# Two joint weight units per feed-forward block: weight loads chained in their written order, and the third weight sum made by VectorE instead of by DMAs

## The chip, the cores and the metric

The kernel runs on one core of a Trainium2 chip. The metric is the device time of one execution in microseconds (us). The program is recorded once, and a scheduler then decides in which order each engine's instructions stand; each engine and each DMA queue works through its own list strictly in that order.

## The reference, cut to what matters

A decoder trunk of four layers on 256 tokens with 1024 channels. Each layer has a feed-forward block (SwiGLU), a token mixer, and a second feed-forward block, so eight feed-forward blocks in all, and these hold most of the weights:

```python
def swiglu(x, wg, wu, wd):
    return (jax.nn.silu(x @ wg) * (x @ wu)) @ wd
...
    for i in range(DEPTH):
        h = rms_norm(x, ffn_norm[i, 0])
        x = x + 0.5 * swiglu(h, ffn_w_gate[i, 0], ffn_w_up[i, 0], ffn_w_down[i, 0])
        ...
        h = rms_norm(x, ffn_norm[i, 1])
        x = x + 0.5 * swiglu(h, ffn_w_gate[i, 1], ffn_w_up[i, 1], ffn_w_down[i, 1])
```

All of it is fp32, with `D_FF` 2816.

## The kernel before, in words

The 256 tokens are two tiles of 128 (t = 0, 1). Weights stream from HBM once. A unit `g` is 512 columns of gate and up weights, and it arrives as two loads of 1 MB (`raw<-gu`); a unit `d` is 512 rows of the down matrix, also two loads of 1 MB (`raw<-dn`). All loads of this kind go through SyncE's DMA queue into three buffers of 1 MB (tag `raw`, `bufs=3`), so a load waits until the last reader of the buffer that it takes over is done, and every later entry of that queue waits behind it.

Each weight is used as two numbers: ScalarE writes the rounded upper part (`hi`), VectorE the rest (`lo` = raw minus hi). That is a split, done in quarters of 128 x 1024, into nine buffers of either kind (`HALVES = 9`); `split_some` hands out the quarters, one or two per tick of the program, and a quarter waits until TensorE has read what its buffers held. Every product is three matmuls (lines 292 to 294, in joint units 474 to 476): hi times upper activations, hi times lower, lo times upper.

The order of units in a block is `FFN_ORDER`: g0 to g3, d0, g4, g5, d1, g6, g7, d2, g8, g9, d3, g10, d5, d4. The pairs (g4, g5) and (g8, g9) are **joint units** (`JOINT = (4, 8,)`): the four weight blocks b11, b21, b12, b22 and both token tiles are multiplied in seven products of half size instead of eight (a Strassen scheme), for which sums of weight blocks are needed:

- t1 = b12 + b11. SyncE loads b12 in two halves (`start`), then GpSimd starts two more DMAs that add b11 to it in flight (`add`, with `accum_op`).
- t2 = t1 + b22, by VectorE in place (line 233).
- t3 = b12 + b22, made like t1 by DMAs: SyncE loads b12 a second time, GpSimd's DMAs add b22.
- t4 = t2 + b21, by VectorE in place over t2.

The sums lie in buffers of tag `a4` (`bufs=9`, half a megabyte each, shared with other tiles). `split_joint` queues the quarters in the order b11, t1, t2, t3, b21, t4, b22; b11, b22 and b21 each hold one of the three `raw` buffers until their last reader is done. `joint` then multiplies: b11, t2, t1, t3, b21, t4, b22.

Behind each joint unit comes a `d` unit, d1 or d3. Its two loads, here called **dn1 and dn2**, take the buffers that b11 and b21 leave. In the scheduled program TensorE multiplies part of that unit for tile 0 (`acc`, lines 292 to 294) after the fifth product and before t4 and b22. The block's values `th` (line 1248 on ScalarE, 1249 on VectorE) and `h` (line 1254) are turned on TensorE (line 1262).

Of the kernel before, what the change touches and what calls it, by code (L numbers as in the profile page):

```python
# [80 lines left out]
class Net:  # L81
    def __init__(self, ctx, tc, a, layers):
        self.tc, self.nc, self.a = tc, tc.nc, a
        self.layers = layers

        def pool(name, **k):
            return ctx.enter_context(tc.tile_pool(name=name, bufs=1, **k))

        self.cp, self.wp, self.ap, self.sp = pool("const"), pool("weights"), pool("act"), pool("small")
        self.ps = pool("psum", space=PSUM)  # L90
        self.units, self.raw, self.parts = [], {}, {}
        self.n_fetch = self.n_split = 0
        self.seq, self.due, self.queue, self.memkv = [], [], [[], []], {}
        self.ticks = 0
        self.jobs, self.open = [], []
        self.extra = []
        self.st, self.splits = [{}, {}], []
        self.plan()
# [30 lines left out]
    def plan(self):  # L129
# [21 lines left out]
        def both(n):  # L151
            self.seq += [(n, 3)] if self.units[n][0] == "j" else [(n, 0), (n, 1)]

        for j, i in enumerate(self.layers):
# [23 lines left out]
            for u in range(n, len(self.units)):  # L178
                both(u)

    def fetch(self):
        u = self.n_fetch
        if u >= len(self.units):
            return
        self.n_fetch += 1
        if self.units[u][0] == "j":
            self.fetch_joint(u)
            return
        self.raw[u] = []
        for ap in self.units[u][1]:  # L190
            n = ap.shape[1]
            r = self.wp.tile([128, n], F32, name="raw", tag="raw", bufs=3)
            self.nc.sync.dma_start(r, ap)
            self.raw[u].append(r)

    def fetch_joint(self, u):

        nc = self.nc
        b11, b21, b12, b22 = self.units[u][1]
        half = lambda ap, q: ap[:, 1024 * q:1024 * q + 1024]  # L200
        raw = self.raw[u] = {}

        def plain(name, ap):
            raw[name] = self.wp.tile([128, 2048], F32, name="raw", tag="raw", bufs=3)
            nc.sync.dma_start(raw[name], ap)

        def start(name):
            raw[name] = [self.t4([128, 1024], "sum") for _ in range(2)]
            for q in range(2):
                nc.sync.dma_start(raw[name][q], half(b12, q))  # L210

        def add(name, ap):
            for q in range(2):
                nc.gpsimd.dma_start(raw[name][q], half(ap, q), accum_op=OP.add)

        plain("b11", b11)
        start("t1")
        add("t1", b11)
        plain("b22", b22)
        start("t3")  # L220
        add("t3", b22)
        plain("b21", b21)

    def split_joint(self, u):
        nc = self.nc
        raw, parts = self.raw.pop(u), self.parts[u]
        parts.update({n: [] for n in ("b11", "t1", "t2", "t3", "b21", "t4", "b22")})
        half = lambda n, q: raw[n][:, 1024 * q:1024 * q + 1024] if n[0] == "b" else raw[n][q]

        def quarter(name, src, q, plus):  # L230
            x = half(src, q)
            if plus:
                nc.vector.tensor_add(x, x, half(plus, q))
            hi = self.wp.tile([128, 1024], F32R, name="hi", tag="hi", bufs=HALVES)
            lo = self.wp.tile([128, 1024], F32R, name="lo", tag="lo", bufs=HALVES)
            nc.scalar.activation(hi, x, AF.Copy)  # L236
            nc.vector.tensor_sub(lo, x, hi.bitcast(F32))  # L237
            parts[name].append((hi, lo))

        for name, src, plus in (("b11", "b11", None), ("t1", "t1", None), ("t2", "t1", "b22"), ("t3", "t3", None),  # L240
                                ("b21", "b21", None), ("t4", "t1", "b21"), ("b22", "b22", None)):
            for q in range(2):
                self.splits.append((u, lambda name=name, src=src, q=q, plus=plus: quarter(name, src, q, plus)))
# [1350 lines left out]
```

## Time and profile before

| | |
|---|---|
| Time, median of 3 runs | 2109.27 us (2106.8 to 2116.53) |
| The profiled execution, own time | 2109.68 us |
| Its span, first to last instruction | 2107.9 us |
| TensorE busy | 2028.5 us (96%) |
| VectorE busy | 1520.9 us (72%) |
| ScalarE busy | 1114.2 us (53%) |
| Moved by DMA | 402.11 MB, mean 191 GB/s |
| TensorE's mean granted clock | 0.985 |

The time of the profiled execution is its span and 1.8 us around it. Matmuls overlap in the pipeline, so a busy TensorE can still be slowed; the number of matmuls in a stretch and the distance from one start to the next tell more than its busy time.

### The profile page before, as it was taken

The page shows a single profiled execution, that of the slowest core. Times are in us where ns is not written, and L with a number is a line of the kernel's source. Part 1 is how long each engine was busy: PE and PEld are TensorE (multiplying, and loading weights), DVE is VectorE, ACT ScalarE, POOL GpSimd, SP SyncE. Part 2 cuts the span into 40 slices and gives each one's busy share as a digit, 9 for nine tenths or more (in the row PEclk, how much of TensorE's full clock was granted, in tenths as well). Part 3 has the DMA queues.
Part 4 walks back from the last instruction along what each step waited for, and adds up shares of the span by engine and source line. Part 5 has one row for each costly group of instructions (what it writes and reads, how often), then busy time and mean ns, then how long its engine had stood idle before and what let it go on. Part 6 is the DMA issues. An engine that isn't in the chain of part 4 may idle for free.

```text
span 2107.9 us, 25369 instructions
## 1 busy us (share of the span) xinstructions
PE 2028.5 (96%) x9486; PEld 1628.5 (77%) x9486; DVE 1520.9 (72%) x2209; ACT 1114.2 (53%) x1562; POOL 227.7 (11%) x349
## 2 busy tenths in 40 slices
PE   8899999899989999989998999999899989999899
PEld 6677777778867887868777788877788778778687
DVE  7677757778767787867777876667786868658675
ACT  6455655446545555545545554544555545545453
POOL 0100411100100022100000112210000100301000
PEclk9999999999999999999999999999999999999999
DMA  7855535865683533684577443137744774436843
GB/s 260 261 189 220 180 120 200 241 218 200 213 245 143 205 110 120 234 246 145 218 235 242 182 173 130 64 121 235 241 179 180 231 248 181 159 120 215 249 149 126
DMA packets 66988, 402.11 MB, mean 191 GB/s; under 512 B 7600, under 2 KB 8016, under 8 KB 28080
## 3 DMA queue, kind: packets, MB, share of 16 engines
q1 hardware_dynamic: 56304, 364.54, 47.2%
q0 software_dynamic: 9408, 33.97, 8.3%
q10 hardware_dynamic: 1152, 1.97, 0.3%
q8 instruction: 75, 1.23, 0.2%
q14 instruction: 49, 0.40, 0.1%
HBM read 399.40 MB, written 1.05 MB: 190 GB/s over the span
## 4 chain that ended last, share of the span: by engine, by line
PE 74%; DMA 12%; DVE 8%; ACT 3%; issue 2%; POOL 1%; SPq 0%; ACTq 0%; DVEq 0%; POOLq 0%
PE pg L292 8%; PE pg L294 8%; PE pg L293 8%; PE acc L293 7%; PE acc L294 6%; PE acc L292 6%; DMA sum<-gu 5%; DVE lo L237 4%; DMA raw<-gu 3%; PE p L292 3%; DMA raw<-dn 3%; PE p L293 3%; PE p L294 3%; DVE lo L265 2%; PE pT L1262 2%
## 5 line engine op out<-in xcount | busy, mean ns | idle before, releaser
L265 DVE TENSOR_TENSOR lo<-raw,hi 128x1024 fp32r<-128x1024 f32 (+3 forms) x516 | 615.6, 1217 | 175.1 <-ACT hi L264 168.5
L264 ACT ACTIVATE hi<-raw 128x1024 fp32r<-128x1024 f32 (+3 forms) x516 | 527.1, 1046 | 273.0 <-DMA raw<-gu 79.0
L292 PE MATMUL pg<-hi,sh 128*128 128x512 f32 x896 | 354.8, 396 | 4.4 <-ACT hi L1347 3.4
L293 PE MATMUL pg<-lo,sh 128*128 128x512 f32 x896 | 350.7, 391 | 0.7 <-DVE lo L1348 0.7
L294 PE MATMUL pg<-hi,sl 128*128 128x512 f32 x896 | 349.8, 390 | 0.0
L292 PE MATMUL acc<-hi,hTh 128*128 128x512 f32 x704 | 286.0, 410 | 34.9 <-ACT hi L264 34.9
L293 PE MATMUL acc<-lo,hTh 128*128 128x512 f32 x704 | 288.0, 413 | 4.6 <-DVE lo L265 4.4
L294 PE MATMUL acc<-hi,hTl 128*128 128x512 f32 x704 | 282.4, 405 | 0.0
L236 ACT ACTIVATE hi<-sum 128x1024 fp32r<-128x1024 f32 x128 | 132.3, 1057 | 165.4 <-PE acc L294 88.9
L237 DVE TENSOR_TENSOR lo<-sum,hi 128x1024 fp32r<-128x1024 f32 x128 | 154.2, 1226 | 77.6 <-ACT hi L236 75.9
L292 PEld LDWEIGHTS pg<-hi,sh 128*128 128x128 f32 x896 | 168.3, 188 | 39.2 <-ACT hi L1347 4.3
L293 PEld LDWEIGHTS pg<-lo,sh 128*128 128x128 f32 x896 | 168.5, 188 | 35.4 <-DVE lo L1348 2.5
L294 PEld LDWEIGHTS pg<-hi,sl 128*128 128x128 f32 x896 | 168.2, 188 | 35.6 <-DVE sl L1370 0.4
L292 PEld LDWEIGHTS acc<-hi,hTh 128*128 128x128 f32 x704 | 135.8, 193 | 68.6 <-ACT hi L264 38.4
L293 PEld LDWEIGHTS acc<-lo,hTh 128*128 128x128 f32 x704 | 136.0, 193 | 42.0 <-DVE lo L265 14.2
L294 PEld LDWEIGHTS acc<-hi,hTl 128*128 128x128 f32 x704 | 136.4, 194 | 27.9 <-DVE hTl L1264 0.2
L1248 ACT ACTIVATE th<-pg,rh 128x256 f32<-128x256 f32 x128 | 60.3, 471 | 179.4 <-PE pg L294 174.0
L1249 DVE SCALAR_TENSOR_TENSOR th<-th,pg 128x256 f32<-128x256 f32 x128 | 53.5, 418 | 107.6 <-ACT th L1248 107.1
L237 DVE TENSOR_TENSOR lo<-raw,hi 128x1024 fp32r<-128x1024 f32 x96 | 114.9, 1226 | 18.9 <-ACT hi L236 18.9
L292 PE MATMUL p<-hi,sh 128*128 128x512 f32 (+4 forms) x320 | 125.2, 391 | 0.3 <-DVE dq_b L529 0.3
L294 PE MATMUL p<-hi,sl 128*128 128x512 f32 (+4 forms) x320 | 121.2, 379 | 0.0
L293 PE MATMUL p<-lo,sh 128*128 128x512 f32 (+4 forms) x320 | 120.9, 378 | 0.0
(344 smaller groups left out, 3185.0 us busy)
## 6 DMA issues: line engine op xcount, KB each, us to landing
raw<-gu SPq DMA_DIRECT2D x158, 1024.0 KB, 5.0
raw<-dn SPq DMA_DIRECT2D x88, 1024.0 KB, 4.9
sum<-gu SPq DMA_DIRECT2D x64, 512.0 KB, 7.6
sum<-gu POOLq DMA_DIRECT2D x64, 512.0 KB, 11.5
raw<-ret SPq DMA_DIRECT2D x20, 1024.0 KB, 4.8
raw<-wout SPq DMA_DIRECT2D x16, 1024.0 KB, 4.8
raw<-mkv SPq DMA_DIRECT2D x8, 1024.0 KB, 4.8
raw<-nsa SPq DMA_DIRECT2D x6, 1024.0 KB, 4.9
```

Of the source, the lines that this page charges most:

```text
L236: nc.scalar.activation(hi, x, AF.Copy)
L237: nc.vector.tensor_sub(lo, x, hi.bitcast(F32))
L264: nc.scalar.activation(hi, src, AF.Copy)
L265: nc.vector.tensor_sub(lo, src, hi.bitcast(F32))
L292: mm(out, ah, bh, start=start, stop=False)
L293: mm(out, ah, bl, start=False, stop=False)
L294: mm(out, al, bh, start=False, stop=stop)
L1248: nc.scalar.activation(th, p[:, :256], AF.Tanh, scale=rh_)
L1249: nc.vector.scalar_tensor_tensor(th, th, 1.0, p[:, :256], op0=OP.add, op1=OP.mult)
L1262: nc.tensor.transpose(c[:, k], h[:, k * 128:k * 128 + 128], self.ident)
```

## The change

Three things are changed. Loads of weights by SyncE go through a helper, `load`, that ties each of them behind the one before, with a dependency that orders the scheduler and makes no semaphore wait. In a joint unit the loads are written in another order (t1's halves first, then b11, b22, b21). And t3 is no longer made by DMAs: VectorE makes it as t2 minus b11, in two instructions of 128 x 1024, into buffers that are allocated when the quarter is split. The order of matmuls is not fixed by anything (the helper `behind` serves loads alone, and `self.last` is not used).

```diff
+        self.last = self.loaded = None
...
+    def load(self, dst, src):
+
+        self.nc.sync.dma_start(dst, src)
+        i = self.nc.cur_bb.bb.instructions[-1]
+        if self.loaded is not None:
+            self.behind(i, self.loaded)
+        self.loaded = i
+
+    def behind(self, i, j):
+
+        self.tc.add_manual_dep(
+            i, j.name, mybir.DependencyInfo(mybir.DependencyClass.NoSync, mybir.DependencyReason.DATA),
+            reason="in order")
...
-            self.nc.sync.dma_start(r, ap)
+            self.load(r, ap)
...
-        plain("b11", b11)
         start("t1")
         add("t1", b11)
+        plain("b11", b11)
         plain("b22", b22)
-        start("t3")
-        add("t3", b22)
         plain("b21", b21)
...
             x = half(src, q)
-            if plus:
+            if name == "t3":
+                raw.setdefault("t3", []).append(self.t4([128, 1024], "sum"))
+                nc.vector.tensor_sub(raw["t3"][q], x, half("b11", q))
+                x = raw["t3"][q]
+            elif plus:
                 nc.vector.tensor_add(x, x, half(plus, q))
...
-        for name, src, plus in (("b11", "b11", None), ("t1", "t1", None), ("t2", "t1", "b22"), ("t3", "t3", None),
+        for name, src, plus in (("b11", "b11", None), ("t1", "t1", None), ("t2", "t1", "b22"), ("t3", "t1", None),
```

**SyncE's queue around the first joint unit of the third feed-forward block (layer 1).** Before (`raw_4701` is b11, `sum_4703` and `sum_4704` t1, `sum_4711` and `sum_4712` t3, `raw_4709` b22, `raw_4717` b21; `raw_4800` and `raw_4802` are dn1 and dn2, and the four `sum_52..` between and behind these are t1 and t3 of the second joint unit):

```order
L205 DMA raw_4701<-gu 128x2048
L210 DMA sum_4703<-gu 128x1024
L210 DMA sum_4704<-gu 128x1024
L210 DMA sum_4711<-gu 128x1024
L210 DMA sum_4712<-gu 128x1024
L205 DMA raw_4709<-gu 128x2048
L205 DMA raw_4717<-gu 128x2048
L193 DMA raw_4800<-dn 128x2048
L210 DMA sum_5225<-gu 128x1024
L210 DMA sum_5226<-gu 128x1024
L210 DMA sum_5233<-gu 128x1024
L193 DMA raw_4802<-dn 128x2048
```

The same place with the change (all of these loads are now recorded at line 184; `sum_4693` and `sum_4694` are t1, `raw_4699`, `raw_4701` and `raw_4703` are b11, b22 and b21, `raw_4786` and `raw_4788` dn1 and dn2, and the last five are the units g6 and g7 and the first load of d2):

```order
L184 DMA sum_4693<-gu 128x1024
L184 DMA sum_4694<-gu 128x1024
L184 DMA raw_4699<-gu 128x2048
L184 DMA raw_4701<-gu 128x2048
L184 DMA raw_4703<-gu 128x2048
L184 DMA raw_4786<-dn 128x2048
L184 DMA raw_4788<-dn 128x2048
L184 DMA raw_4893<-gu 128x2048
L184 DMA raw_4895<-gu 128x2048
L184 DMA raw_5096<-gu 128x2048
L184 DMA raw_5098<-gu 128x2048
L184 DMA raw_5139<-dn 128x2048
```

The four loads for the second joint unit have left their places around dn2. Two of them are gone, and the other two stand behind both loads of d2, directly ahead of the second unit's b11:

```order
L184 DMA raw_5141<-dn 128x2048
L184 DMA sum_5213<-gu 128x1024
L184 DMA sum_5214<-gu 128x1024
L184 DMA raw_5219<-gu 128x2048
L184 DMA raw_5221<-gu 128x2048
```

(`raw_5141` is the second load of d2, `sum_5213` and `sum_5214` are t1 of the second joint unit, the two behind them its b11 and b22; GpSimd's queue has two additions per joint unit, and had four.)

**VectorE at the same joint unit.** Before (L233 adds b22 or b21 to t1, L237 writes a lower part, `hTl` belongs to the block's activations):

```order
L237 TENSOR_TENSOR lo_4881<-sum_4703,hi_4880 128x1024
L233 TENSOR_TENSOR sum_4704<-sum_4704,raw_4709 128x1024
L1264 TENSOR_TENSOR hTl_4849<-pT_4872,hTh_4848 128x512
L233 TENSOR_TENSOR sum_4703<-sum_4703,raw_4717 128x1024
L237 TENSOR_TENSOR lo_4886<-sum_4704,hi_4885 128x1024
L237 TENSOR_TENSOR lo_4902<-sum_4711,hi_4901 128x1024
L237 TENSOR_TENSOR lo_4924<-sum_4712,hi_4923 128x1024
```

With the change (lines 250 and 254 are 233 and 237 of before, 1281 is 1264; line 247 is the subtraction):

```order
L254 TENSOR_TENSOR lo_4867<-sum_4693,hi_4866 128x1024
L250 TENSOR_TENSOR sum_4694<-sum_4694,raw_4701 128x1024
L1281 TENSOR_TENSOR hTl_4835<-pT_4858,hTh_4834 128x512
L247 TENSOR_TENSOR sum_4887<-sum_4693,raw_4699 128x1024
L247 TENSOR_TENSOR sum_4911<-sum_4694,raw_4699 128x1024
L250 TENSOR_TENSOR sum_4693<-sum_4693,raw_4703 128x1024
L254 TENSOR_TENSOR lo_4872<-sum_4694,hi_4871 128x1024
```

Both subtractions stand ahead of the first addition of b21, and everything behind them keeps its order. They are the last readers of b11's buffer, which dn1 takes over. TensorE's list keeps its order but for some exchanges among `acc` matmuls and transposes behind a joint unit.

## Rows read from the trace of the kernel before

**Rows 1.** The page: the length of the profiled execution, and its first part, the busy time of each engine with its share of the span and its number of instructions.

```profile
span 2107.9 us, 25369 instructions
...
PE 2028.5 (96%) x9486; PEld 1628.5 (77%) x9486; DVE 1520.9 (72%) x2209; ACT 1114.2 (53%) x1562; POOL 227.7 (11%) x349
```

**Rows 2.** The waits of TensorE over the whole span. Columns: engine, what it was to write and the line, the engine and line that it waited for, then the total in us, how often, and the longest one in us.

```profile
PE acc L292 <- ACT hi L264: 34.9, 8, 5.7
PE pT L1262 <- DVE h L1254: 20.7, 15, 5.1
PE acc L293 <- DVE lo L265: 4.4, 12, 0.5
```

**Rows 3.** The timeline of TensorE at the first joint unit of the third feed-forward block (layer 1). Columns: start in us, duration in us, engine, line, operation, output and inputs, count; in brackets the idle time just before and what ended it.

```profile
589.02 0.44 PE L1262 MATMUL pT<-ident,h 128*128 128x128 f32 x2 [2.00 <-DVE h L1254]
...
612.31 0.40 PE L294 MATMUL acc<-hi,hTl 128*128 128x512 f32 x1
618.19 0.80 PE L292 MATMUL acc<-hi,hTh 128*128 128x512 f32 x1 [5.48 <-ACT hi L264]
619.45 0.80 PE L293 MATMUL acc<-lo,hTh 128*128 128x512 f32 x1 [0.47 <-DVE lo L265]
...
623.03 0.42 PE L474 MATMUL pg<-hi,op 128*128 128x512 f32 x1
```

**Rows 4.** The same joint unit in stretches of 10 us. Columns: stretch, its length, then for each engine the busy time with the number of instructions, then the granted TensorE clock, the share of the DMA engines and GB/s.

```profile
600.00:610.00 10.00, 10.00 (x45) 8.23 (x44) 9.39 (x10) 6.84 (x8) 1.73 (x2) 1.00 0.82 206
610.00:620.00 10.00, 4.06 (x14) 2.67 (x13) 3.54 (x4) 2.37 (x3) 0.86 (x1) 0.81 1.04 315
620.00:630.00 10.00, 10.00 (x38) 8.00 (x37) 7.87 (x13) 5.05 (x6) 0.86 (x1) 0.85 1.03 352
```

**Rows 5.** The span of the core and its mean granted TensorE clock over the whole execution (1 is the upper of its two levels).

```profile
core 0: 2107.9 us, clock 0.985
```

**Rows 6.** The DMA queue of SyncE around both joint units of that block, the starts of its DMAs. The duration of a merged row reaches from the first start to the end of the last issue.

```profile
562.94 2.24 SPq L210 DMA_DIRECT2D sum<-gu  x4
...
581.69 0.33 SPq L193 DMA_DIRECT2D raw<-dn  x1
599.09 4.87 SPq L210 DMA_DIRECT2D sum<-gu  x3
604.76 0.33 SPq L193 DMA_DIRECT2D raw<-dn  x1
...
631.99 7.00 SPq L193 DMA_DIRECT2D raw<-dn  x2
...
658.42 21.75 SPq L193 DMA_DIRECT2D raw<-dn  x2
```

**Rows 7.** The DMAs that GpSimd starts there (the additions in flight).

```profile
571.38 0.87 POOL L214 DMA_DIRECT2D sum<-gu  x1 [0.34 <-DVE lo L265]
...
603.43 0.86 POOL L214 DMA_DIRECT2D sum<-gu  x1 [28.70 <-DMA sum<-gu]
605.77 0.87 POOL L214 DMA_DIRECT2D sum<-gu  x1 [1.48 <-DVE s L488]
```

**Rows 8.** The timeline of ScalarE there: the upper parts of weights (`hi`) and, at 586.53, a tanh of the block.

```profile
585.57 1.06 ACT L236 ACTIVATE hi<-sum 128x1024 fp32r<-128x1024 f32 x1 [3.33 <-DMA sum<-gu]
586.53 0.46 ACT L1248 ACTIVATE th<-pg,rh 128x256 f32<-128x256 f32 x1
...
607.71 1.99 ACT L264 ACTIVATE hi<-raw 128x1024 fp32r<-128x1024 f32 x2
617.08 2.00 ACT L264 ACTIVATE hi<-raw 128x1024 fp32r<-128x1024 f32 x2 [7.37 <-DMA raw<-dn]
...
657.38 1.06 ACT L236 ACTIVATE hi<-sum 128x1024 fp32r<-128x1024 f32 x1 [0.25 <-PE pg L294]
...
659.20 1.06 ACT L236 ACTIVATE hi<-sum 128x1024 fp32r<-128x1024 f32 x1 [0.27 <-PE pg L294]
...
682.75 3.89 ACT L264 ACTIVATE hi<-raw 128x1024 fp32r<-128x1024 f32 x4
```

**Rows 9.** The timeline of VectorE there: additions to the sums (L233) and the lower parts of weights (`lo`, L237).

```profile
591.76 1.22 DVE L233 TENSOR_TENSOR sum<-sum,raw 128x1024 f32<-128x1024 f32 x1
596.70 3.50 DVE L237 TENSOR_TENSOR lo<-sum,hi 128x1024 fp32r<-128x1024 f32 x3 [3.72 <-ACT hi L236]
...
603.51 1.22 DVE L233 TENSOR_TENSOR sum<-sum,raw 128x1024 f32<-128x1024 f32 x1
...
671.20 3.50 DVE L237 TENSOR_TENSOR lo<-sum,hi 128x1024 fp32r<-128x1024 f32 x3 [3.90 <-ACT hi L236]
```

**Rows 10.** The page, its sixth part: DMAs by output, source and issuing engine; count, KB of each, and the median time in us from issue to landing.

```profile
raw<-dn SPq DMA_DIRECT2D x88, 1024.0 KB, 4.9
sum<-gu SPq DMA_DIRECT2D x64, 512.0 KB, 7.6
sum<-gu POOLq DMA_DIRECT2D x64, 512.0 KB, 11.5
```

**Rows 11.** The same landings with their spread, for the additions that GpSimd starts.

```profile
DMA to landing us min/median/max: 8.2/11.5/19.4
```

**Rows 12.** The timeline of TensorE at the second joint unit of the same block.

```profile
687.40 0.40 PE L292 MATMUL acc<-hi,hTh 128*128 128x512 f32 x1
687.94 0.50 PE L293 MATMUL acc<-lo,hTh 128*128 128x512 f32 x1
```

More of the change, by code (lines that the diff above doesn't have):

```diff
@@ L204, in plain @@
             raw[name] = self.wp.tile([128, 2048], F32, name="raw", tag="raw", bufs=3)
-            nc.sync.dma_start(raw[name], ap)
+            self.load(raw[name], ap)
         def start(name):
@@ L209, in start @@
             for q in range(2):
-                nc.sync.dma_start(raw[name][q], half(b12, q))
+                self.load(raw[name][q], half(b12, q))
         def add(name, ap):
```

## The prediction

> **What bounds the kernel now.** I read the busy times first: TensorE works in 96% of the span, VectorE in 72% and ScalarE in 53% [rows 1]. So a microsecond counts only where TensorE itself stands still or is slowed, and the next view is the list of its waits. Three entries there bear on this change: the multiplication of a `dn` unit waits 34.9 us for upper parts of weights (8 times, one for each feed-forward block, mean 4.4), then 4.4 us for lower parts, and the transposes wait 20.7 us for `h` (15 times, mean 1.38) [rows 2]. The rest of TensorE's time is matmuls, whose number the change leaves alone.
>
> The timeline of one block shows where this happens. At its first joint unit TensorE ends a matmul at 612.71 and starts the next one at 618.19, 5.48 us later, because ScalarE has not written `hi`; after one matmul it waits 0.47 us more for `lo` [rows 3]. Nine matmuls then run from 618.19 to 623.03, in 4.84 us. In an undisturbed stretch 45 of them take 10 us, 0.222 us each, at a granted clock of 1.00; around the stall the clock is 0.81 and 0.85, a mean over the upper level and half of it [rows 4]. Nine at 0.222 us are 2.0 us, so beyond the 0.47 us of waiting, 2.4 us are lost to the clock that fell after the stall. Over eight blocks that is 19 us, and it fits under what the whole execution can have lost: a mean clock of 0.985 over 2107.9 us [rows 5] leaves 31.6 us.
>
> Why is `hi` late? ScalarE did the quarters of dn1 at 607.71, then waited 7.37 us for dn2's transfer, until 617.08 [rows 8]. dn2 was issued at 604.76 [rows 6], right after VectorE's addition of b21 ended at 604.73 (603.51 and 1.22) and freed the buffer [rows 9]. It took 12.3 us to land, against a median of 4.9 for loads of its kind [rows 10]. Around it the queues carry the four loads for the second joint unit's sums, hoisted to here: three issued from 599.09 [rows 6], with GpSimd's additions at 603.43 and 605.77 behind them [rows 7]; the DMA engines are full, at 1.04 [rows 4]. The comparison is the second joint unit of the same block, which has no foreign loads around its dn2. There the last issue ends at 680.17 (658.42 and 21.75) [rows 6], ScalarE goes through all four quarters from 682.75 without a wait [rows 8], and TensorE's two matmuls start 0.54 us apart [rows 12], 0.3 more than 0.222.
>
> The second stall begins with t1. Its loads are issued from 562.94 [rows 6], the addition at 571.38 [rows 7], and ScalarE gets the sum at 585.57, after 3.33 us of waiting; the `tanh` behind it starts late [rows 8], and with it `h`: TensorE waits 2.00 us at 589.02 [rows 3]. So 1.3 us of that lateness were slack.
>
> **The change part by part.**
>
> *The chain itself* makes no semaphore wait and costs no engine anything. Its effect is the new order of SyncE's queue: behind dn1 and dn2 come g6, g7 and d2, and t1 of the second joint unit only after these.
>
> *t3's transfers.* Of 64 loads by SyncE and 64 additions by GpSimd, 512 KB each [rows 10], half go: 64 transfers fewer, of 32 MB in all. GpSimd is no bound (11% [rows 1]); what counts is that nothing of this kind is in flight at dn2.
>
> *t3 on VectorE* costs two subtractions per joint unit, 32 in all. The nearest row is the addition of the same shape, 1.22 us [rows 9], so 39 us of VectorE. At the place where they now stand, behind the second addition of b22 (ending at 592.98), VectorE idled 3.72 us for ScalarE's `hi`; in the second joint unit 3.90 us [rows 9]. Two subtractions are 2.44 us, and fit. The bounds are 0 (all in idle time) and 39 us (all on the path). I take 0, because both idles exceed the price.
>
> *dn1 waits longer.* b11's buffer is now free only after the second subtraction, at about 595.4, where dn1 was issued at 581.69 [rows 6]. With 4.9 us it lands at 600.3; ScalarE wants it at 607.71 [rows 8], so 7.4 us of cover are left. Behind it in the queue dn2 waits, whose buffer comes free at 604.7 as before. Cost 0.
>
> *dn2.* Issued at 604.8 and landing after 4.9 us it is there at 609.7, just when ScalarE has done dn1 (607.71 and 1.99). TensorE started 1.11 us after ScalarE's start (618.19 against 617.08), which now makes 610.8, and it is busy until 612.71. So the 5.48 us go, with 1.9 us to spare, and as no stall remains, the clock stays up. The low bound is that all 34.9, 4.4 and 19 us go, the high that dn2 lands no sooner than now. I take the second joint unit's state: 0.3 us left per block, 2.4 us in all.
>
> *t1 of the first joint unit* is issued ahead of b11 instead of behind it, and t3's four transfers no longer run beside its additions. Of the 15 waits for `h` I let the eight at the first joint units go and keep seven at the mean of 1.38: 9.7 us stay, 11.0 go. (Bounds: 0 and 20.7.)
>
> *t1 of the second joint unit* loses its early place. d2's second load starts at 638.66 (631.99 + 7.00 − 0.33) [rows 6]; with 7.6 us for the load, 0.9 for GpSimd's issue [rows 7] and 11.5 for the addition [rows 10] the sum lands at 658.7 to 659.0, where ScalarE wants its first half at 657.38 [rows 8]. That is up to 1.6 us late, less the 1.3 of slack seen above: 0.3. I take 0.5 us per block, 4 us. The low bound is 0 (the shortest addition, 8.2 [rows 11], comes in time); the high one is below.
>
> Here a rule speaks against the change. The trace has t1's loads some 58 us ahead of their use (599.09 to 657.38 [rows 6, 8]), and ScalarE doesn't wait for them. The Trainium skill, "DMA: Bandwidth & Descriptors", section "Rules for kernel authors", says to issue a DMA early and to wait on it late, so that its setup is overlapped; the change issues these later. By that rule the late t1 would cost what the rival of that name gives, 2064, instead of the 2047 of the sum by rows; the trace of before agrees with it for t1, but shows its price at dn2.
>
> **The sum.** At stake are 34.9 + 4.4 + 20.7 + 19 = 79 us. Kept: 2.4 + 9.7 + 4 = 16. The profiled execution took 2109.68 us (2107.9 of span and 1.8 around it), practically the median of 2109.27. 2109.7 − 63 = **2047 us**.
>
> **The rivals.**
>
> *Second joint unit's t1 late.* If it lands as the first one's does now, 22.6 us after its first issue (562.94 to 585.57), it is there at 661.3, 3.9 us late; less 1.3 that is a stall of 2.6, in eight blocks 21 us in place of 4: 2043 + 21 = 2064. For it: the same chain of two transfers. Against it: the four transfers of t3 that ran beside it are gone.
>
> *VectorE on the path.* If the idle before `lo` was only the shadow of work that now moves up, all 39 us count: 2047 + 39 = 2086. For it: 72% busy, and the subtractions stand ahead of the t4 addition that frees dn2's buffer. Against: the idle of 3.72 and 3.90 us at this very place.
>
> *The change doesn't do what it says.* dn2's 12.3 us are a matter of the gu loads behind it, which fill the DMA engines as well. Then only t1's part is gained, 11 − 4 = 7: 2103. Against: dn2 of the second joint unit.
>
> *Slower.* t1 of the second joint unit lands at the long end: 638.66 + 7.6 + 0.9 + 19.4 [rows 11] = 666.6, 9.2 us late, stalling TensorE 7.9 us and losing another 2.4 to the clock: 8 × 10.3 = 82, 2043 + 82 = 2125. It decides for slower when the lateness exceeds 8.6 us in every block (a stall of 7.3). Against: 19.4 is the longest of 64.
>
> **How the numbers follow.** Forecast 0.62 (its own range 2033 to 2062, from nearly all of the 79 us gone to t1 almost as late as in the rival), second t1 late 0.15, VectorE on the path 0.10, no effect at dn2 0.08, slower 0.05. 0.5% is 10.5 us, about what a measurement of this kernel can tell from no change; 2103 lies within it and 2125 beyond. Faster: 0.62 + 0.15 + 0.10 = 0.87; same 0.08; slower 0.05. The range leaves out the last two: from 2028, a little below the floor of 2031 that all 79 us would give, to 2088, which takes in VectorE on the path.
>
> **What would show it.** In the profile after, the wait of `acc` for `hi` of a `dn` unit is down from 34.9 to a few us and dn2 of the first joint unit lands in about 5 us; the mean clock rises to 0.99 or more; SyncE and GpSimd have 32 DMAs to `sum` each; the subtractions lie in what was idle time before `lo`, and the idle before the t4 additions does not move. A wait of ScalarE for `sum` at the second joint unit, with a wait for `h` behind it, would show the first rival or the slower case, by its length. Wrong I would be if dn2 landed late although nothing for sums is in flight, or if the stall moved from dn2 to dn1, now that dn1 waits for the subtraction.

## The result, and the profile after

| | before | after |
|---|---|---|
| Time, median | 2109.91 us (2106.8 to 2116.53) | 2038.2 us (2034.82 to 2039.38) |
| The profiled execution: own time, span | 2109.68, 2107.9 us | 2034.82, 2033.0 us |
| TensorE busy | 2028.5 us | 2004.1 us |
| TensorE's mean granted clock | 0.985 | 0.998 |

The ratio of the times is 0.966, 95% interval 0.964 to 0.968: 72 us or 3.4% less. The profiled execution after is the shortest of its four runs, so its trace shows some 3 us less than the median.

The page after answers to [rows 1] and [rows 10]. First its span and busy times, then its DMAs to the buffers that matter here (count, KB of each, median us from issue to landing):

```profile
span 2033.0 us, 25241 instructions
PE 2004.1 (99%) x9486; PEld 1615.2 (79%) x9486; DVE 1554.8 (76%) x2241; ACT 1114.5 (55%) x1562; POOL 198.5 (10%) x317
...
raw<-dn SPq DMA_DIRECT2D x88, 1024.0 KB, 4.8
sum<-gu SPq DMA_DIRECT2D x32, 512.0 KB, 7.0
sum<-gu POOLq DMA_DIRECT2D x32, 512.0 KB, 9.5
```

The number of matmuls is the same and VectorE works 34 us more, yet TensorE is busy 24.4 us less: the same matmuls, run at a higher clock. The waits of TensorE after (columns as in [rows 2]):

```profile
PE pT L1279 <- DVE h L1271: 9.3, 6, 4.1
...
PE acc L310 <- DVE lo L282: 0.3, 2, 0.2
```

The wait of `acc` for upper parts of a `dn` unit, 34.9 us in [rows 2], is not in the list any more; that for lower parts went from 4.4 to 0.3 us, that for `h` from 20.7 to 9.3 us. Those three make 50.4 us, and the 24.4 us of busy time make 74.8: that is the whole difference of the spans, 74.9 us.

The first joint unit of the same block after, SyncE's queue, VectorE and ScalarE (they answer to [rows 6], [rows 9] and [rows 8]; the block now begins some 19 us earlier):

```profile
576.52 11.11 SPq L184 DMA_DIRECT2D raw<-dn  x2
...
574.11 2.35 DVE L247 TENSOR_TENSOR sum<-sum,raw 128x1024 f32<-128x1024 f32 x2
576.38 1.22 DVE L250 TENSOR_TENSOR sum<-sum,raw 128x1024 f32<-128x1024 f32 x1
579.20 3.50 DVE L254 TENSOR_TENSOR lo<-sum,hi 128x1024 fp32r<-128x1024 f32 x3 [1.60 <-ACT hi L253]
...
590.22 3.89 ACT L281 ACTIVATE hi<-raw 128x1024 fp32r<-128x1024 f32 x4
```

dn1 is issued at 576.52, right behind the second subtraction (574.11 and 2.35). dn2 is issued at 587.30 (576.52 + 11.11 − 0.33), and ScalarE goes through dn1's and dn2's four quarters in one piece, so dn2 was there by 592.2, at most 4.9 us after its issue instead of 12.3. The two subtractions take 2.35 us, and VectorE's idle time ahead of `lo` shrank from 3.72 to 1.60 us.

What is left of the wait for `h`: 4.06 us in the first block, and 5.2 us in five second joint units. The first block's, the longest of the five, and ScalarE's wait for t1's second half in the third block, where TensorE has none over 0.5 us:

```profile
69.71 0.49 PE L1279 MATMUL pT<-ident,h 128*128 128x128 f32 x2 [4.06 <-DVE h L1271]
1672.26 0.44 PE L1279 MATMUL pT<-ident,h 128*128 128x128 f32 x2 [1.41 <-DVE h L1271]
...
633.38 1.06 ACT L253 ACTIVATE hi<-sum 128x1024 fp32r<-128x1024 f32 x1 [0.98 <-DMA sum<-gu]
```

In that third block t1 is now just late.

### The profile page after: what moved, and what is told of

It reads as the page before. It is cut to its first block, busy times and chain, and to the rows that moved or that the text cites. A ratio compares the mean times of both kernels' runs of the same rounds, so it can differ in the third digit from the quotient of the medians.

```text
span 2033.0 us, 25241 instructions
## 1 busy us (share of the span) xinstructions
PE 2004.1 (99%) x9486; PEld 1615.2 (79%) x9486; DVE 1554.8 (76%) x2241; ACT 1114.5 (55%) x1562; POOL 198.5 (10%) x317
## 4 chain that ended last, share of the span: by engine, by line
PE 87%; DMA 5%; DVE 4%; ACT 1%; issue 1%; POOL 1%; SPq 0%; ACTq 0%; POOLq 0%; DVEq 0%
PE pg L309 8%; PE pg L311 8%; PE pg L310 8%; PE acc L310 8%; PE acc L311 8%; PE acc L309 8%; DMA sum<-gu 4%; PE pg L492 3%; PE pg L491 3%; PE pg L493 3%; PE p L309 3%; PE p L310 3%; PE p L311 3%; PE pT L1279 2%; PE pT L564 1%; PE po L309 1%
## 5 line engine op out<-in xcount | busy, mean ns | idle before, releaser
L310 PE MATMUL acc<-lo,hTh 128*128 128x512 f32 x704 | 281.1, 403 | 0.5 <-DVE lo L282 0.3
L309 PE MATMUL acc<-hi,hTh 128*128 128x512 f32 x704 | 278.1, 399 | 0.0
```

The lines of the kernel that those rows point to most:

```text
L309: mm(out, ah, bh, start=start, stop=False)
L310: mm(out, ah, bl, start=False, stop=False)
```

## The experiments

The kernel before was timed again beside each group of them, with medians of 2110.8, 2112.0 and 2112.9 us; every ratio is to these. Theory: dn2 was late because transfers for the second joint unit's sums were in flight around it; the chain takes them away, and making t3 on VectorE makes it affordable that t1 comes later. Rivals: the gain is that of half the sum traffic; what delays dn2 are the gu loads behind it; VectorE's subtractions cost something that other gains cover.

**One part alone: the chain.** t3 by DMAs, in the old written order, with `load` kept:

```diff
+        plain("b11", b11)
         start("t1")
         add("t1", b11)
-        plain("b11", b11)
         plain("b22", b22)
+        start("t3")
+        add("t3", b22)
         plain("b21", b21)
...
```

> The chained loads alone: t3 is still made by DMAs (64 loads and 64 additions to sums, as before), in the old written order, b11 first. Theory A (dn2 was late because foreign sum loads stand before and beside it in the queues): the wait of acc for the upper parts of dn units falls from 34.9 us to under 3, with its 4.4 us for lower parts and about 17 us of clock; the second joint unit's t1 and t3 are issued behind d2 and come late, some 2 us in each of eight blocks: 2110 - 56 + 16, about 2070 us. Theory B (the gain comes from the halved traffic, not from the order): dn2 stays late, 2100 to 2110 us.

Measured: 2087.6 us (2085.0 to 2089.9), ratio 0.988 (0.985 to 0.992). The first line of TensorE's waits, and one of the places:

```profile
PE pT L1277 <- DVE h L1269: 45.0, 9, 9.7
...
657.78 0.44 PE L1277 MATMUL pT<-ident,h 128*128 128x128 f32 x2 [4.52 <-DVE h L1269]
```

No wait for the parts of a `dn` unit is in the list any more: the chain mends dn2 with all of the sum traffic still there, so the traffic theory falls for dn2. But 45 us of waiting for `h` have come: nearly 10 in the first block, and 3.8 to 5 in the second joint unit of each of the eight, where t1 is late. I had put 2 there. About half of what the chain gives goes into this. The four transfers of t3 run beside t1's additions here, and b11 is loaded ahead of t1; the run further down that has this b11 order without t3's transfers waits 18.0 us for `h`, so by that comparison some 27 of the 45 come with t3's transfers.

**The other part alone: t3 on VectorE.** No chain, the old written order:

```diff
-        start("t3")
-        add("t3", b22)
...
+            if name == "t3":
+                raw.setdefault("t3", []).append(self.t4([128, 1024], "sum"))
+                nc.vector.tensor_sub(raw["t3"][q], x, half("b11", q))
...
```

> t3 by VectorE alone: no chain, the old written order. In the scheduled queue two sum loads (t1 of the second joint unit) still stand between dn1 and dn2, where there were three or four. Theory A: dn2 is late by about half of the 7.4 us of before, it lands 8 to 9 us after its issue and TensorE waits 1.5 to 2.5 us per block; 2053 to 2070 us. Theory B (halved traffic is what counts): dn2 lands in 5 us, the time is that of the changed kernel, about 2038 us. Rival C (one foreign load is as bad as four): the 34.9 us stay, about 2100 us.

Measured: 2073.8 us (2069.8 to 2076.9), ratio 0.982 (0.979 to 0.985). TensorE's waits, then GpSimd's queue, SyncE's and ScalarE around dn2 in the same joint unit:

```profile
PE acc L294 <- ACT hi L266: 21.4, 8, 4.2
...
599.36 0.86 POOL L214 DMA_DIRECT2D sum<-gu  x1 [30.21 <-DVE lo L239]
601.31 0.86 POOL L214 DMA_DIRECT2D sum<-gu  x1 [1.09 <-DVE s L490]
...
600.33 0.33 SPq L193 DMA_DIRECT2D raw<-dn  x1
...
610.84 2.00 ACT L266 ACTIVATE hi<-raw 128x1024 fp32r<-128x1024 f32 x2 [5.61 <-DMA raw<-dn]
```

Here t1's two halves are still hoisted to dn2's place. dn2 lands after 10.5 us (600.33 to 610.84), later than the 8 to 9 expected, and 21.4 of the 34.9 us stay. So halving the traffic is not enough while it lies at this place. The parts alone give 23 and 37 us, together 72: the chain is worth more when t3's transfers don't make t1 late.

**What makes dn2 late: traffic behind it in its own queue?** The changed kernel, with four copies of 512 KB to memory that nothing reads, directly behind dn2:

```diff
...
             self.load(r, ap)
             self.raw[u].append(r)
+            if u + 4 < len(self.units) and self.units[u - 1][0] == self.units[u + 4][0] == "j" and len(self.raw[u]) == 2:
+                for q in range(4):
+                    x = self.hp.tile([128, 1024], F32, name="idle", tag="idle", bufs=8)
+                    self.load(x, self.units[u + 4][1][2 - 2 * (q // 2)][:, 1024 * (q % 2):1024 * (q % 2) + 1024])
```

> The changed kernel with four foreign copies of 512 KB (to memory that nothing reads) issued directly behind dn2 of every first joint unit. Theory (traffic beside dn2 made it late, wherever it stands in the queue): dn2 lands after 8 to 12 us in place of 4.8, the wait of acc for the upper parts of dn units comes back with 3 to 6 us and the clock falls, 8 x 5.5 to 9 us: 2082 to 2110 us. Rival (a load is served ahead of those issued behind it): dn2 still lands in 5 us, no such wait; only the units behind it can be late, 2038 to 2060 us.

Measured: 2056.2 us (2051.7 to 2061.3), ratio 0.975 (0.972 to 0.977). SyncE's queue and ScalarE at the joint unit:

```profile
593.76 0.33 SPq L185 DMA_DIRECT2D raw<-dn  x1
594.14 0.50 SPq L185 DMA_DIRECT2D idle<-gu  x1
...
596.68 3.98 ACT L286 ACTIVATE hi<-raw 128x1024 fp32r<-128x1024 f32 x4
```

My expectation was wrong and the rival right. 2 MB were issued from 0.4 us behind dn2 on, and dn2's quarters still follow dn1's without a wait: it landed within 4.9 us (593.76 to 598.7). The 18 us came from elsewhere: TensorE's wait for `h` is 23.0 us in place of 9.3, and its busy time 9.5 us more; the scheduler also ordered the matmuls behind the joint unit anew. That also speaks against a rival of the prediction, that the gu loads behind dn2 were its cause. (The copies go to memory and the gu loads to buffers on the core; but in the kernel before, the gu loads were issued later, from 609.47 on, 4.7 us behind dn2, and in the changed kernel they again follow at 4.7 us: 591.97 behind 587.30.)

**Traffic of the other queue, with and without adding.** GpSimd starts two transfers onto t4's sum once it is used up, so that they fall near where the hoisted additions fell (0.9 us ahead of dn2's issue and 2.7 behind it; in the kernel before 1.3 ahead and 1.0 behind). All other engines keep their order, entry by entry:

```diff
             parts[name].append((hi, lo))
+            if name == "t4" and u + 5 < len(self.units) and self.units[u + 5][0] == "j":
+                nc.gpsimd.dma_start(x, self.units[u][1][0][:, 1024 * q:1024 * q + 1024], accum_op=OP.add)
```

In the second of the two kernels `accum_op` is left off.

> The changed kernel with two additions of 512 KB by GpSimd's DMAs, onto the two halves of t4's sum once both parts of it are written (so nothing that is used changes), at every first joint unit: they start within about 1 us before and 2.5 us after dn2's issue, as before; the orders of TensorE, ScalarE, VectorE and SyncE's queue are the same, entry by entry. Theory (the additions of the other queue made dn2 late, since copies behind it in its own queue didn't): dn2 lands after 8 to 11 us, the wait of acc for the upper parts of dn units comes back with 2 to 5 us a block, and the clock falls: 2060 to 2095 us. Rival (the sum loads ahead of dn2 in SyncE's queue made it late): no such wait, 2038 us.

> As the run with the additions, but the two transfers are plain loads of the same 512 KB by GpSimd's queue, without adding. If it is the other queue's share of the DMA engines that counts: dn2 as late as with the additions, the same time. If it is the adding: less, dn2 in 6 to 7.5 us, a wait under 1 us a block, 2038 to 2048 us.

Measured: with additions 2077.8 us (2075.3 to 2083.4), ratio 0.983 (0.980 to 0.986); with plain loads 2049.4 us (2048.1 to 2052.2), ratio 0.969 (0.967 to 0.972). With additions, GpSimd's queue, dn2's issue, ScalarE, TensorE behind it, and TensorE's waits:

```profile
597.53 0.86 POOL L257 DMA_DIRECT2D sum<-gu  x1 [33.36 <-DVE lo L254]
601.10 0.86 POOL L257 DMA_DIRECT2D sum<-gu  x1 [2.71 <-DVE lo L254]
...
598.44 0.33 SPq L184 DMA_DIRECT2D raw<-dn  x1
...
607.68 2.00 ACT L283 ACTIVATE hi<-raw 128x1024 fp32r<-128x1024 f32 x2 [4.33 <-DMA raw<-dn]
...
608.79 0.80 PE L311 MATMUL acc<-hi,hTh 128*128 128x512 f32 x1 [2.47 <-ACT hi L283]
...
PE acc L311 <- ACT hi L283: 15.4, 8, 2.5
PE acc L312 <- DVE lo L284: 5.8, 10, 0.8
```

With plain loads, ScalarE at dn2's quarters, and TensorE behind it:

```profile
601.21 2.01 ACT L283 ACTIVATE hi<-raw 128x1024 fp32r<-128x1024 f32 x2 [2.15 <-DMA raw<-dn]
...
602.32 0.50 PE L311 MATMUL acc<-hi,hTh 128*128 128x512 f32 x1 [0.29 <-ACT hi L283]
```

dn2 lands after 9.2 us beside two additions (598.44 to 607.68), 7.1 beside two plain loads of the same size (issued at 594.14 = 583.36 + 11.11 − 0.33 of that queue), 4.9 beside neither. The Trainium skill, "DMA: Bandwidth & Descriptors", section "Issuing engines are not separate DMA queues", says that transfers of SyncE and GpSimd run on the same 16 engines and interleave; the plain loads agree with it. The additions cost dn2 twice what the plain loads do, 4.3 us and 2.2, so both the sharing and the adding count. Of the 7.4 us that dn2 was late before, 4.3 are shown so. The other 3.1 are not shown; nearest are the sum loads ahead of it in SyncE's queue, the last issued at about 603.6, 1.1 us before dn2 [rows 6]. In the run with t3 on VectorE two such loads stood ahead of dn2 besides the two additions, and dn2 took 10.5 us, 1.3 more than here; a run with such loads ahead of dn2 alone was not made.

These two runs also measure TensorE's margin at dn2. ScalarE waited 4.33 and 2.15 us there, TensorE 2.47 and 0.29: 1.9 us were covered both times, as the prediction had it.

The stall also prices the clock. With additions TensorE waits only some 2.6 us in each block for `hi` and `lo` together, and its busy time is 2024.0 us, 19.9 more than in the changed kernel. In the 10 us from the end of each of the eight stalls the granted clock is 0.67, 0.68 or, six times, 0.83, which makes 16.7 us, 2.1 a block, not far from the waiting itself; the rest of the 19.9 lies elsewhere. The third block's stretch (columns as in [rows 4]):

```profile
608.79:618.79 10.00, 9.54 (x29) 7.27 (x30) 7.12 (x9) 4.48 (x6) 0.00 (x0) 0.67 0.73 285
```

**The price of the subtractions.** Each is written twice over in one kernel, left out in another:

```diff
                 nc.vector.tensor_sub(raw["t3"][q], x, half("b11", q))
+                nc.vector.tensor_sub(raw["t3"][q], x, half("b11", q))
```

> The changed kernel with each subtraction for t3 written twice over, 32 more on VectorE, 39 us of its time. If they lie in idle time (1.6 us of idle is left ahead of the lower parts behind them, against 2.4 us more): at most 0.8 us later at dn2, which has slack: 2038 to 2043 us. If VectorE is on the path there: 2038 + 39 = 2077 us.

> The changed kernel with the subtraction for t3 left out (t3 takes t1's values, so that part of the product is not computed): no instruction for t3's making is left anywhere. If the subtractions are hidden, as the doubled ones suggested, 2038 us or, like the doubled ones, up to 13 us away from it in either direction by what the scheduler makes of it. If they are on the path: 2038 - 39 = 1999 us.

Measured: twice 2025.5 us (2022.8 to 2029.0), left out 2023.3 us (2023.1 to 2034.0). Both are faster than the changed kernel, and 2.2 us from each other, so neither number is the price of a subtraction: the scheduler ordered TensorE and ScalarE anew in both. With four of them VectorE's idle time ahead of `lo` is used up to the last, and nothing more:

```profile
575.04 2.35 DVE L248 TENSOR_TENSOR sum<-sum,raw 128x1024 f32<-128x1024 f32 x2
577.32 1.21 DVE L251 TENSOR_TENSOR sum<-sum,raw 128x1024 f32<-128x1024 f32 x1
578.45 3.49 DVE L255 TENSOR_TENSOR lo<-sum,hi 128x1024 fp32r<-128x1024 f32 x3
```

VectorE was not the bound: with 32 us more of busy time on it (1587.2 against 1554.8) the kernel did not get slower. What the new orders gave can be seen in part. d2's loads and t1's of the second joint unit in SyncE's queue, first of the changed kernel, then with the subtractions twice:

```profile
604.23 8.36 SPq L184 DMA_DIRECT2D raw<-dn  x2
612.64 0.90 SPq L184 DMA_DIRECT2D sum<-gu  x2
```

```profile
603.84 6.79 SPq L184 DMA_DIRECT2D raw<-dn  x2
610.69 0.90 SPq L184 DMA_DIRECT2D sum<-gu  x2
```

ScalarE splits the unit ahead of d2 earlier there, d2's second load gets its buffer sooner, and t1, behind it, is issued 1.95 us earlier (612.64 and 610.69). The waits for `h` are down to 4.0 us in all, the first block's. The rest of the difference stays open.

**t1 earlier.** Is that lateness what is left to gain? t1's loads and additions are written ahead of d2, and TensorE, ScalarE, VectorE and GpSimd keep their order, entry by entry:

```diff
         for ap in self.units[u][1]:
...
+            if u + 1 < len(self.units) and self.units[u - 4][0] == self.units[u + 1][0] == "j" and not self.raw[u]:
+                self.early(u + 1)
             self.load(r, ap)
...
```

`early` does what `start` and `add` do for t1, and `fetch_joint` leaves that out when it is done.

> The changed kernel with the loads and additions of t1 for the second joint unit moved ahead of d2 in the queues; the order of TensorE, ScalarE and VectorE is the same, entry by entry. Theory: of the 9.3 us that TensorE still waits for h, the 5.2 us in five second joint units come from t1 landing late; with some 8 us more of lead they go, and the clock has nothing more to give back: 5 us faster than the changed kernel, about 2033 us. Rival: d2's loads are pushed back and come late in its place; a wait for the upper parts of a dn unit appears, 2040 us or more.

Measured: 2027.8 us (2027.7 to 2029.3), ratio 0.961 (0.960 to 0.963), 10 us or 0.5% under the changed kernel. Its waits for `h`, and the place in the third block where d2 is late in return:

```profile
PE pT L1281 <- DVE h L1273: 5.2, 1, 5.2
...
621.05 2.01 ACT L283 ACTIVATE hi<-raw 128x1024 fp32r<-128x1024 f32 x2 [3.43 <-DMA raw<-dn]
```

The five waits are gone and only the first block's is left. d2's second load does come 3.43 us late for ScalarE, as the rival had it, but TensorE has no wait for it. Between the profiled executions the spans differ by 7.0 us (2033.0 and 2026.0), of which the five waits explain 5.2 and a slightly longer one in the first block takes 1.2 back; 1.4 us are TensorE's busy time, and the rest and the 3 us beyond, between the medians, were not traced.

With t1 ahead of the `d` unit for both joint units (the same edit with the condition widened):

> The changed kernel with t1 ahead of the d unit for both joint units of a block. Over the version that does it for the second one alone (2028 us) it can gain the last wait for h, 5.2 us in the first block; in the other blocks t1 of the first joint unit is in time already: 2023 us if that goes. Rival: the scheduler orders the first block anew, 2028 us or some us away from it either way.

Measured: 2026.2 us (2023.6 to 2028.0), ratio 0.958 (0.955 to 0.961): the first block's wait of 5.2 us is gone too, but 2.5 us of waiting for `h` stand there at another matmul, with the first block's order changed a little, and two second joint units wait 1.2 us together. The time cannot be told from that of the kernel with one t1 moved. These two are faster than both kernels of the case.

**The third part undone.** b11 ahead of t1 again:

```diff
-        start("t1")
-        add("t1", b11)
         plain("b11", b11)
+        start("t1")
+        add("t1", b11)
```

> The changed kernel with b11 loaded ahead of t1 again, the third part of the change undone alone. In the queue of the second joint unit t1 then waits for b11's buffer. Theory: t1 comes later by that wait (b11 was issued some 1 us behind t1 there) and by a share of b11's traffic, 1 to 3 us in each second joint unit: 2046 to 2062 us. Rival: this part does nothing, 2038 us.

Measured: 2046.6 us (2045.9 to 2049.2), ratio 0.970 (0.968 to 0.972), at the lower end of what was expected and 8 us above the changed kernel. ScalarE waits for t1's two halves in the second joint unit of the third block, 1.78 us in place of none and 1.00 in place of 0.98:

```profile
638.18 1.06 ACT L253 ACTIVATE hi<-sum 128x1024 fp32r<-128x1024 f32 x1 [1.78 <-DMA sum<-gu]
640.72 1.06 ACT L253 ACTIVATE hi<-sum 128x1024 fp32r<-128x1024 f32 x1 [1.00 <-DMA sum<-gu]
```

TensorE's waits for `h` are 18.0 us in place of 9.3: 6.5 in the first block, and 11.4 in the second joint units, now of all eight blocks. So the written order of b11 and t1 matters where t1 has no slack. The order of some matmuls differs from the changed kernel's too, but those 8.7 us of waiting cover the 8 us.

**A late dn2 that the scheduler knows of.** dn2 loaded twice into the same buffer, the second load behind the first's landing:

```diff
             self.load(r, ap)
+            if self.units[u - 1][0] == "j" and self.raw[u]:
+                self.load(r, ap)
```

> The changed kernel with the second load of d1 and d3 made twice into the same buffer, the second behind the first's landing: dn2 arrives about 5 us later in 16 joint units, with no other traffic added. If TensorE has the 1.9 us of margin that was worked out, it stands still for about 3.3 us, and with a clock that falls it loses 2.4 to 3.3 us more: 16 x 5.7 to 6.6, 2129 to 2144 us. Without a price in clock: 16 x 3.3, 2091 us. With 5 us of margin or more: 2038 us.

Measured: 2038.4 us (2036.6 to 2041.3), ratio 0.966 (0.962 to 0.969): the changed kernel's time, so all three numbers for a stall were wrong here. The fourth, 2038, came true, but not for its reason, a margin of 5 us. The load did come late, but TensorE had other work:

```profile
595.97 2.01 ACT L283 ACTIVATE hi<-raw 128x1024 fp32r<-128x1024 f32 x2 [2.67 <-DMA raw<-dn]
```

With the second load in the program, the scheduler put t4's and b22's products ahead of most of dn's matmuls. The run says nothing of TensorE's margin, for which it was made; the runs with transfers beside dn2 do. It does say that a delay in the scheduler's view need cost nothing; the delay from the other queue's additions, which fell on an order that had dn's matmuls first, cost up to 5.7 us a block [rows 2].

## Why the prediction was right

It forecast 2047 us, with 2033 to 2062 for its likeliest case; 2038.2 was measured. The mechanism is the one described, with dn2's cause narrowed by the runs, and most terms can be read off the trace after.

- **dn2.** Expected: issued as before, landing after 4.9 us, no stall but for 0.3 us a block. Found: landing by 4.9 us, and of 34.9 and 4.4 us only 0.3 in all is left, so the 2.4 us kept were too much. The 1.9 us to spare are what the two runs with transfers beside dn2 show.
- **What made dn2 late.** I named the hoisted loads and additions together, with the DMA engines full. The runs separate them: the other queue's additions make about 4.3 of 7.4 us, and transfers behind dn2 in its own queue nothing. So busy DMA engines alone were not the cause. The other 3.1 us stay open.
- **dn1's new wait.** Issued at 576.5 behind the second subtraction, 13.7 us before ScalarE begins on it (590.22). The cover was there, at no cost.
- **The subtractions.** Expected 0 out of bounds of 0 and 39 us; they lie in VectorE's idle time, and TensorE waits 0.3 us in all for `lo` of a `dn` unit. The rival with VectorE on the path falls; doubled, they made the kernel no slower, though with matmuls in a new order.
- **t1 of the second joint unit.** Expected 0.5 us a block, 4 us; found 5.2 us in five blocks. In the third block it is t1's second half that ScalarE waits for, 20.7 us after the first issue (612.64 to 633.38), where 20.3 were reckoned; that wait of 0.98 us cost TensorE nothing, as the slack of 1.3 us had it. The rival's 22.6 us are a second half's too (585.57), but were set against 657.38, where ScalarE wants the first; the second is wanted at 659.20 [rows 8], so the rival had 2.1 us of lateness and not 3.9, which makes it some 2049 in place of 2064. The rivals in which it comes later still did not happen in the changed kernel, but the chain alone, with t3's transfers beside t1, shows how near they were: there it cost 3.8 to 5 us in each of eight blocks.
- **The wait for `h`, mis-sized.** I kept 9.7 us of the old waits and 4 us of new ones, 13.7 together; 9.3 are left. The seven waits that I kept were taken by count and mean, without looking where they stand. In the trace before, eight waits stand at the first joint units, 13.6 us in all, and seven 14 to 17 us behind the stall at dn2 (in the first block a short one), 7.1 us. Those seven, which were to stay, went with the stall; of the eight, which were to go, the first block's stayed. What is left is the first block's 4.06 us and the second joint units' 5.2, which I had counted under another name already.
- **The clock, mis-sized.** Expected 8 × 2.4 = 19 us, found 24.4. One block's loss was taken for all eight, and it was the smallest: by the granted clock of the 10 us behind each stall the seven long ones lost 2.4 to 3.4 us, 20.7 together (the first block's stall was 0.77 us, with no lower clock behind it). Two further stretches at half the clock went that were not counted, one in the first block behind a wait for `h`, one far from any joint unit; at 0.83 over 10 us they make 1.7 us each, and 20.7 and 3.4 are 24.1. Before, behind the stalls of the third and the seventh block, and the two further stretches (columns as in [rows 4]); then the first of these two after:

```profile
618.19:628.19 10.00, 9.54 (x32) 7.28 (x33) 7.87 (x10) 4.96 (x7) 0.86 (x1) 0.76 1.03 350
1691.46:1701.46 10.00, 9.54 (x28) 7.30 (x29) 6.74 (x9) 3.29 (x4) 0.86 (x1) 0.66 1.04 356
110.00:120.00 10.00, 9.62 (x39) 7.68 (x40) 6.79 (x11) 5.71 (x8) 1.69 (x2) 0.83 0.75 241
1370.00:1380.00 10.00, 10.00 (x56) 8.18 (x55) 5.19 (x14) 5.74 (x9) 0.82 (x2) 0.83 0.50 195
```

```profile
110.00:120.00 10.00, 10.00 (x46) 8.24 (x45) 6.56 (x8) 5.37 (x7) 0.78 (x1) 1.00 0.68 245
```

Why the clock fell in the stretch far from any joint unit stays open.

These terms close the sum: 63 us were forecast, and with 2.1 (dn2), 4.4 (`h`) and 5.4 (clock) more it is 74.9, the difference of the spans. All three errors had the same sign, so the forecast didn't come near by errors that cancel.

The rule weighed in the prediction (the Trainium skill, "DMA: Bandwidth & Descriptors", section "Rules for kernel authors"), that DMAs be issued early, bore on t1 after all: issued ahead of d2 it gave 10 us more. It is not early or late as such that decided but what a transfer lies beside: hoisted to dn2 it cost more than it saved.

## What to carry to other kernels

A transfer that comes late is to be read together with what the other queue does in those microseconds, and a transfer that a scheduler moves early is to be followed to its new neighbours. Two changes that each give a part can give more together, when the second removes what the first one makes late: here 23 and 37 us alone, 72 together. Where a scheduler orders the engines, a difference of half a per cent between two versions is only evidence when the orders have been compared; the runs that kept every engine's order are the ones that told causes apart most clearly here.

## What the runs showed of the hardware

- Two additions of 512 KB from GpSimd's queue took dn2's landing from 4.9 to 9.2 us, plain loads in their place to 7.1. In the 2 us that begin 1.5 us after GpSimd's issue, with dn2's load under way as well, the DMA engines were as busy with additions as with plain loads, 1.02 and 0.95, but moved half as much, 125 GB/s and 248. The rows (columns as in [rows 4]), with additions and with plain loads:

```profile
599.03:601.03 2.00, 2.00 (x10) 1.63 (x10) 1.45 (x2) 2.00 (x3) 0.00 (x0) 1.00 1.02 125
```

```profile
594.75:596.75 2.00, 2.00 (x10) 1.63 (x9) 1.46 (x2) 2.00 (x3) 0.00 (x0) 1.00 0.95 248
```

- Copies of 2 MB issued directly behind a load in the same queue did not delay it: it landed within 4.9 us.
- Short stalls had the lower clock behind them here. In the run with additions, TensorE's matmuls behind a wait of 2.47 us (up to 608.79), with one of 0.46 us behind it, still start 0.42 us apart five microseconds later, and 0.24 us from 615.33 on. Behind the changed kernel's wait of 1.41 us (up to 1672.26) the granted clock stayed at the upper level. The rows, of the run with additions and of the changed kernel:

```profile
613.63 0.63 PE L493 MATMUL pg<-hi,op 128*128 128x512 f32 x1
614.05 0.63 PE L494 MATMUL pg<-lo,op 128*128 128x512 f32 x1
...
615.33 0.40 PE L494 MATMUL pg<-lo,op 128*128 128x512 f32 x1
615.57 0.39 PE L495 MATMUL pg<-hi,op 128*128 128x512 f32 x1
```

```profile
1672.26:1682.26 10.00, 10.00 (x44) 8.17 (x45) 8.56 (x9) 4.03 (x5) 0.00 (x0) 1.00 0.29 105
```
